# A 128-byte pad ahead of the difference tiles of the four late seven-product stages of a hybrid encoder block

## The chip, the cores and the metric

The kernel runs on one core of a Trainium2 chip. The metric is device time in microseconds (us), the median of several executions. One more execution was recorded by the hardware profiler; every row of a trace below is of that one, and places in it are given in us from its first instruction. The engines are TensorE (PE in the rows; its weight loads are PEld), VectorE (DVE), ScalarE (ACT), GpSimd (POOL) and SyncE (SP, which issues most transfers).

## The reference

One encoder layer over 1024 positions of 1024 channels, with 16 learned meta positions ahead of them, all in float32:

```
u = rms_norm(h, pre_w)
z = u @ w_in                          # 1024 x 7680: q, k, v, gates of both branches
y_r = gated(retention(rq, rk, rv), rg) @ w_ret_branch
y_a = gated(window_attention(aq, ak, av), ag) @ w_attn_branch
out = (sigmoid(gr) * y_r + sigmoid(ga) * y_a) @ w_out
return h + rms_norm(out, post_w)
```

Retention is bidirectional over chunks of 128 with 4 heads; attention sees a window of 128 on both sides, the meta positions and a learned sink.

## The kernel before, in words

**Precision.** Every operand of a large product is held as two tiles, a high part (ScalarE casts it to the fast float32 form) and a low part (VectorE subtracts the high part from the source). The helper `mm3` (lines 93 to 98) makes one product of a 128x128 block out of three matmuls: high weights by high moving data (line 95), low weights by high moving data (line 96), high weights by low moving data (line 97). So a row of line 95, 96 or 97 is one third of a block product, and each of them reads 512 float32 columns, 2048 bytes in each partition, of its moving operand:

```
def mm3(o, ah, al, bh, bl, first, last, free_group=False):
    kw = {"skip_group_check": True} if free_group else {}
    nc.tensor.matmul(o, ah, bh, start=first, stop=False, **kw)
    nc.tensor.matmul(o, al, bh, start=False, stop=False, **kw)
    latest[:] = [nc.tensor.matmul(o, ah, bl, start=False, stop=last, **kw).ins]
```

**Seven products.** The large projections are done in 2x2 blocks with seven products instead of eight. Four of the seven moving operands are plain blocks or a difference kept in the tile `big` (B11, B21, B22 and T1); three are differences of blocks that have tiles of their own, T2, T3 and T4 (`PROD`, line 969). Each of the three has a high and a low tile of 128 partitions by 4 rows (index k) by 512 columns, 8192 bytes in each partition. A product runs four values of k, three matmuls each, so 12 matmuls; units (256 output channels) are taken in pairs, so that the same moving operand serves 24 matmuls in a row, or 12 where pairs are interleaved (`sequence`, line 1166, and `Phase.product`, line 1071).

**Stages.** An early stage `y` (line 1710; the rows have `by`, and its difference tiles are called `T2q`, `T3q` and `T4q`, made by `products`, line 514) runs from about 340 to 500 us. Then comes attention, with single products of the next stage as filler between its steps (rows `pe`). The four late stages follow one another in `steps` (line 1477): `z` (rows `bz`; the remaining gate projections, 12 units), `r` (rows `br`; the retention branch's projection, 4 units), `a` (rows `ba`; the attention branch's, 4 units) and `o` (rows `bo`; the output projection, 4 units). All four use one set of T2, T3 and T4 tiles, which are filled anew for each: by transfers that bring back what stage `y` stored (`get_sum`, line 1178), by ScalarE and VectorE (`split_b`, line 1662, called from `refill`, line 1188), or by transfers of sums that were made earlier (`get_pre`, line 1174).

**What sets the order.** `run` (line 1272) prepares the weights (`lh`, `ll`) up to six products ahead; each engine's instructions are in one fixed order, settled when the program is built. VectorE adds the products up out of PSUM (rows `c1`, `u2`, `u3`, `c5`; line 1111), applies factors (lines 1323, 1362), and makes the low parts (line 111).

**Where the tiles lie.** After attention its pools are closed, and three pools are opened on the space that they leave. `gp` has the buffers of fetched data and of small results (`gtile`, line 981: six buffers of 2048 bytes, and eight small ones for the last norm); `yt`, right behind it, has the six difference tiles:

```
yp, gp, yt = (ctx.enter_context(tc.tile_pool(name=n, bufs=1, reuse_waits="tile")) for n in ("yp", "gp", "yt"))
for n in ("T2", "T3", "T4"):
    B[n] = [yt.tile([P, 4, 512], R, name=f"{n}{s}")[:, :, :] for s in range(2)]
for n in ("T2", "T3", "T4"):
    get_sum(n)
    next(steps)
```

The built program gives each tile a byte address, the same in every partition. The tiles that the argument is about are these (s = 0 is the high tile, s = 1 the low one; the four k rows of a T tile lie 2048 bytes apart, so all four have the same remainder):

| tile | address of s = 0 | address of s = 1 | remainder mod 256 |
|---|---|---|---|
| T2 (stages z, r, a, o) | 122720 | 130912 | 96 |
| T3 | 139104 | 147296 | 96 |
| T4 | 155488 | 163680 | 96 |
| T4q (stage y) | 131040 | 139232 | 224 |
| T3q | 147424 | 155616 | 224 |
| T2q | 163808 | 172000 | 224 |
| big, B11 | 6816 | 40096 | 160, then 224, 32, 96 with k |
| weights, high and low, of stage y and of the late stages | 172000 and up | 184288 and up | 224 |

Of the kernel before, what the change touches and what calls it, by code (L numbers as in the profile page):

```python
# [7 lines left out]
F32 = mybir.dt.float32  # L8
# [8 lines left out]
P = 128  # L17
# [39 lines left out]
def block_kernel(ctx: ExitStack, tc: tile.TileContext, xT, x, meta, w_in, w_rb, w_ab, w_out, vecs, dec, sink,  # L57
# [1743 lines left out]
    rope_stack.close()  # L1801
    free.extend(["p1", "p1", "p3"])
    yp, gp, yt = (ctx.enter_context(tc.tile_pool(name=n, bufs=1, reuse_waits="tile")) for n in ("yp", "gp", "yt"))
    for n in ("T2", "T3", "T4"):
        B[n] = [yt.tile([P, 4, 512], R, name=f"{n}{s}")[:, :, :] for s in range(2)]
    for n in ("T2", "T3", "T4"):
# [86 lines left out]
```

## Time and profile before

| | us |
|---|---|
| median of 3 executions | 1047.75 |
| lowest and highest of them | 1047.32, 1048.1 |
| the profiled execution's own time | 1047.21 |
| its span, first to last instruction | 1045.4 |

The span is what the rows add up to; 1.8 us of the profiled execution lie around it. The granted TensorE clock is 0.996 of full speed on average. In the windows view, a stretch of the span is followed by each engine's busy time in it with the number of instructions, then the granted clock (PEclk), the mean busy share of the DMA engines and GB/s. A row of the timeline has the start and the duration of one instruction. Matmuls are pipelined: each lasts about 0.39 us in the rows, though the next one starts some 0.23 us after it, so what a matmul costs is read from the distance between starts, not from its duration. I call that distance the **step**.

### The profile page before, as it was taken

The page shows a single profiled execution, that of the slowest core. Times are in us where ns is not written, and L with a number is a line of the kernel's source. Part 1 is how long each engine was busy: PE and PEld are TensorE (multiplying, and loading weights), DVE is VectorE, ACT ScalarE, POOL GpSimd, SP SyncE. Part 2 cuts the span into 40 slices and gives each one's busy share as a digit, 9 for nine tenths or more (in the row PEclk, how much of TensorE's full clock was granted, in tenths as well). Part 3 has the DMA queues.
Part 4 walks back from the last instruction along what each step waited for, and adds up shares of the span by engine and source line. Part 5 has one row for each costly group of instructions (what it writes and reads, how often), then busy time and mean ns, then how long its engine had stood idle before and what let it go on. Part 6 is the DMA issues. An engine that isn't in the chain of part 4 may idle for free. (4 is left out here: it accounts for less than half of the span.)

```text
span 1045.4 us, 17242 instructions
## 1 busy us (share of the span) xinstructions
PE 1028.3 (98%) x5797; PEld 892.6 (85%) x5797; DVE 844.4 (81%) x1739; ACT 511.9 (49%) x1118; POOL 210.1 (20%) x274
## 2 busy tenths in 40 slices
PE   9999999999999999999899999999999999999997
PEld 8998999989999888888699898888888888787886
DVE  7887788779889787895877886699899799768766
ACT  5641441423435643433677776476567355333432
POOL 4424235235233002331023331000000000111030
PEclk9999999999999999999899999999999999999999
DMA  9322211215244399997976784999889747789472
GB/s 342 156 81 91 82 42 51 72 36 197 77 142 143 120 409 323 267 290 231 325 215 215 240 248 150 361 382 344 301 291 345 243 137 256 207 227 323 108 139 101
DMA packets 117961, 217.17 MB, mean 208 GB/s; under 512 B 12704, under 2 KB 44352, under 8 KB 115280
## 3 DMA queue, kind: packets, MB, share of 16 engines
q1 hardware_dynamic: 112144, 206.09, 57.3%
q0 software_dynamic: 5440, 9.44, 6.1%
q8 instruction: 46, 0.75, 0.3%
q10 hardware_dynamic: 288, 0.53, 0.2%
q14 instruction: 43, 0.35, 0.1%
HBM read 142.57 MB, written 75.55 MB: 209 GB/s over the span
## 5 line engine op out<-in xcount | busy, mean ns | idle before, releaser
L95 PE MATMUL pv<-wh,big 128*128 128x256 f32 x256 | 73.3, 286 | 0.0
L96 PE MATMUL pv<-wh,big 128*128 128x256 f32 x256 | 72.9, 285 | 0.0
L97 PE MATMUL pv<-wl,big 128*128 128x256 f32 x256 | 72.5, 283 | 0.0
L1548 POOL TENSOR_SCALAR p<-p,den 128x352 f32<-128x352 f32 (+2 forms) x56 | 36.3, 661 | 126.2 <-DVE den L1541 53.0
L1371 POOL DMA_DIRECT2D mx_d<-c1a x4 | 3.5, 872 | 287.3 <-DVE c1a L1362 287.3
L95 PE MATMUL bz<-T,lhz 128*128 128x512 f32 x144 | 56.8, 395 | 0.0
L96 PE MATMUL bz<-T,llz 128*128 128x512 f32 x144 | 56.8, 394 | 0.0
L97 PE MATMUL bz<-T,lhz 128*128 128x512 f32 x144 | 56.8, 394 | 0.0
L1014 ACT CAST why<-wry 128x512 fp32r<-128x512 f32 x56 | 33.0, 620 | 47.3 <-PE by L97 26.2
L96 PE MATMUL by<-big,wly 128*128 128x512 f32 x128 | 50.7, 396 | 0.0
L95 PE MATMUL by<-big,why 128*128 128x512 f32 x128 | 50.4, 394 | 0.0
L97 PE MATMUL by<-big,why 128*128 128x512 f32 x128 | 50.4, 393 | 0.0
L96 PEld LDWEIGHTS pv<-wh,big 128*128 128x128 f32 x256 | 48.2, 188 | 0.3
L95 PEld LDWEIGHTS pv<-wh,big 128*128 128x128 f32 x256 | 48.2, 188 | 0.2
L97 PEld LDWEIGHTS pv<-wl,big 128*128 128x128 f32 x256 | 48.3, 189 | 0.2
L1463 POOL DMA_DIRECT2D aq_d<-m_aq x32 | 27.2, 1278 | 104.0 <-DVE u3y L1458 66.1
L111 DVE TENSOR_TENSOR wly<-wry,why 128x512 fp32r<-128x512 f32 x56 | 38.0, 694 | 11.3 <-ACT why L1014 11.2
L1538 ACT ACTIVATE p<-raw,nm 128x353 f32<-128x353 f32 (+2 forms) x64 | 36.2, 567 | 15.5 <-DVE nm L1535 14.6
L596 ACT ACTIVATE op<-pa,rcol 128x256 f32<-128x256 f32 x32 | 15.3, 477 | 41.9 <-PE pa L97 41.6
L658 ACT ACTIVATE ost<-to,rnw 128x128 f32<-128x128 f32 x64 | 20.1, 366 | 31.4 <-PE to L653 21.8
L1535 DVE CUSTOM_DVE_ANT_0 raw<-ps,mask,nsink 128x352 f32<-128x352 f32 (+2 forms) x64 | 33.2, 548 | 2.7 <-ACT p L1538 1.9
L689 POOL TENSOR_TENSOR rs<-rs,mhalf 128x1 f32<-128x1 f32 x32 | 23.3, 727 | 52.5 <-DVE rs L688 49.2
(715 smaller groups left out, 3768.0 us busy)
## 6 DMA issues: line engine op xcount, KB each, us to landing
e<-e SPq DMA_DIRECT2D x60, 256.0 KB, 5.2
we<-in_w_in_dram SPq DMA_DIRECT2D x20, 512.0 KB, 5.5
wr<-in_w_in_dram SPq DMA_DIRECT2D x19, 512.0 KB, 4.2
wry<-in_w_in_dram SPq DMA_DIRECT2D x16, 512.0 KB, 6.9
tg<-tg_d SPq DMA_DIRECT2D x32, 256.0 KB, 5.0
T<-tT SPq DMA_DIRECT2D x6, 1024.0 KB, 10.3
T<-preT SPq DMA_DIRECT2D x6, 1024.0 KB, 7.1
wrz<-in_w_in_dram SPq DMA_DIRECT2D x20, 256.0 KB, 5.3
```

The lines of the kernel that those rows point to most:

```text
L95: nc.tensor.matmul(o, ah, bh, start=first, stop=False, **kw)
L96: nc.tensor.matmul(o, al, bh, start=False, stop=False, **kw)
L97: latest[:] = [nc.tensor.matmul(o, ah, bl, start=False, stop=last, **kw).ins]
L111: return nc.vector.tensor_tensor(o, i, hi.bitcast(F32), ALU.subtract).ins
L596: nc.scalar.activation(o, pa[:, 0:256], AF.Copy, scale=rcol[:, c:c + 1])
L658: nc.scalar.activation(ost[0][:, e_, w0:w0 + P], to[:, P * e_:P * e_ + P], AF.Copy, scale=rnw[:, 2 * h + e_:2 * h + e_ + 1])
L689: nc.gpsimd.tensor_tensor(rs, rs, mhalf[:, 0:1], ALU.pow)
L1014: nc.scalar.copy(h, src)
L1463: nc.gpsimd.dma_start(d[a], m2[b], accum_op=ALU.add)
L1535: nc.vector.tensor_tensor_reduce(raw[e_][:, 1:1 + wid], s[:, 0:wid], mask[:, mo:mo + wid], -SCALE, nsink[:, hp:hp + 1], ALU.add, ALU.min, ...
L1538: last["exp"] = nc.scalar.activation(p[:, 0:1 + wid], raw[e_][:, 0:1 + wid], AF.Exp, scale=-1.0, bias=nm_[:, e_:e_ + 1], accum_out=den[:, ...
L1548: nc.gpsimd.tensor_scalar(pt[e_][:, 0:wid], pt[e_][:, 0:wid], den[:, e_:e_ + 1], 1.0, op0=ALU.mult, op1=ALU.mult)
```

## The change

One tile of 128 bytes in each partition is taken from the pool `gp` ahead of everything else in it. Nothing reads or writes it.

```
@@ -1801,6 +1801,7 @@
     rope_stack.close()
     free.extend(["p1", "p1", "p3"])
     yp, gp, yt = (ctx.enter_context(tc.tile_pool(name=n, bufs=1, reuse_waits="tile")) for n in ("yp", "gp", "yt"))
+    gp.tile([P, 32], F32, name="pad")
     for n in ("T2", "T3", "T4"):
         B[n] = [yt.tile([P, 4, 512], R, name=f"{n}{s}")[:, :, :] for s in range(2)]
     for n in ("T2", "T3", "T4"):
```

In the built program the change moves no instruction: all five engines have the same instructions in the same order, with the same waits for the same counts. What differs is the address of 20 buffers, each 128 bytes higher: the six buffers of `gtile` (110176 to 120416 before, 110304 to 120544 now), the eight small ones behind them, and the six difference tiles. Those start now at 122848, 131040 (T2), 139232, 147424 (T3), 155616 and 163808 (T4), all at 224 mod 256. Five of these six are, to the byte, the starts of tiles of T2q, T3q and T4q in the table above. The weights, `big`, the tiles of the other pools and everything in PSUM stay where they were.

More of the change, by code (lines that the diff above doesn't have):

```diff
@@ L1803, in block_kernel @@
     yp, gp, yt = (ctx.enter_context(tc.tile_pool(name=n, bufs=1, reuse_waits="tile")) for n in ("yp", "gp", "yt"))
+    gp.tile([P, 32], F32, name="pad")
     for n in ("T2", "T3", "T4"):
```

## Prediction

> **What bounds the kernel now.** I read the page first, then the waits of PE from 660 us to the end, where the four late stages lie, then the windows.
>
> ```profile
> span 1045.4 us, 17242 instructions
> PE 1028.3 (98%) x5797; PEld 892.6 (85%) x5797; DVE 844.4 (81%) x1739; ACT 511.9 (49%) x1118; POOL 210.1 (20%) x274
> ```
> ```profile
> PE bo L95 <- ACT lho L1014: 0.8, 1, 0.8
> ```
> ```profile
> 700.00:740.00 40.00, 40.00 (x174) 32.41 (x173) 36.89 (x61) 22.96 (x43) 0.00 (x0) 1.00 0.96 330
> 780.00:820.00 40.00, 40.00 (x174) 32.40 (x173) 36.18 (x60) 27.51 (x51) 0.00 (x0) 1.00 0.96 338
> 846.00:892.00 46.00, 46.00 (x199) 37.09 (x199) 45.98 (x77) 26.36 (x48) 0.00 (x0) 1.00 0.55 180
> ```
>
> From 660 us on PE has a single listed wait, 0.8 us. In the windows (PE, PEld, DVE, ACT, POOL, then the clock) PE is busy throughout at clock 1.00. So matmuls set the end there, and only what changes the step between matmuls can change the time. The third window is special: DVE is busy for 45.98 of 46.00 us, so there DVE sets the pace too.
>
> **How many matmuls read the moved tiles.** The groups with `T` as moving operand, line 95 (lines 96 and 97 have the same counts):
>
> ```profile
> L95 PE MATMUL bz<-T,lhz 128*128 128x512 f32 x144 | 56.8, 395 | 0.0
> L95 PE MATMUL br<-T,lhr 128*128 128x512 f32 x48 | 18.9, 394 | 0.0
> L95 PE MATMUL ba<-T,lha 128*128 128x512 f32 x48 | 18.9, 394 | 0.0
> L95 PE MATMUL bo<-T,lho 128*128 128x512 f32 x44 | 17.2, 394 | 0.0
> ```
>
> That is 3 x (144 + 48 + 48 + 44) = 852. The durations say nothing of the step, so I take starts from the timeline. First the tiles as they lie now (96 mod 256): the first, eleventh and last row of a run of T matmuls in stage z, and the `big` row behind a run.
>
> ```profile
> 719.21 0.39 PE L95 MATMUL bz<-T,lhz 128*128 128x512 f32 x1
> 721.53 0.40 PE L96 MATMUL bz<-T,llz 128*128 128x512 f32 x1
> 727.58 0.39 PE L95 MATMUL bz<-big,lhz 128*128 128x512 f32 x1
> ...
> 763.81 0.39 PE L95 MATMUL bz<-T,lhz 128*128 128x512 f32 x1
> 772.21 0.39 PE L95 MATMUL bz<-big,lhz 128*128 128x512 f32 x1
> ```
>
> The first run has 36 matmuls. Its first ten take 2.32 us, a step of 232 ns; the other 26 take 6.05 us, a step of 232.7 ns. Another run of 36 takes 8.40 us, 233.3 ns each. Now stage y, whose tiles lie at 224 mod 256, where the change puts the late ones:
>
> ```profile
> 403.45 0.39 PE L95 MATMUL by<-T3q,why 128*128 128x512 f32 x1
> 405.76 0.39 PE L96 MATMUL by<-T3q,wly 128*128 128x512 f32 x1
> 408.94 0.39 PE L95 MATMUL by<-big,why 128*128 128x512 f32 x1
> ...
> 491.78 0.39 PE L95 MATMUL by<-T4q,why 128*128 128x512 f32 x1
> 494.50 0.40 PE L97 MATMUL by<-big,why 128*128 128x512 f32 x1
> ```
>
> Here the first ten of the T3q run of 24 take 2.31 us, 231 ns each, and the other 14 take 3.18 us, 227 ns each. The T4q run of 12, which follows a single `big` matmul, takes 2.72 us, 226.7 ns each from its first on. So these tiles have a shorter step, after some ten matmuls in which it settles. Over all rows of T2q to T4q from 350 us to 494 us, counted by their place in the run, the first ten average 230.1 ns and the later ones 226.7. The late T rows, from 674.59 to 1035.32 us, average 232.0 and 232.6.
>
> The clock and the transfers do not separate the two (windows of PE alone: busy time, clock, DMA share, GB/s):
>
> ```profile
> 403.45:408.94 5.49, 5.49 (x26) 1.00 1.01 328
> 719.21:727.58 8.37, 8.37 (x38) 1.00 1.02 369
> ```
>
> The clock is 1.00 and the DMA share 1.01 and 1.02. The matmuls' shape and the remainder of the weights' addresses are alike too. What differs is the start of the moving operand, and the change makes that equal: five of the six tiles come to lie on the very bytes of T?q tiles. The peculiar pace of each address I can't explain, only read.
>
> **The sum.** A T matmul at its eleventh place or later should save 232.6 - 226.7 = 5.9 ns. One of the first ten should save 232.0 - 230.1 = 1.9 ns; the two runs shown bound that by 1.0 (231 against 232) and 5.3 (226.7 against 232). Counted so, 423 of the 852 are late in their run and 429 early: 423 x 5.9 + 429 x 1.9 = 3.3 us if nothing takes it back. Two stretches do.
>
> The first is 846 to 893 us:
>
> ```profile
> DVE llr L111 <- PE br L96: 1.3, 1, 1.3
> ```
> ```profile
> PEld ba L96 <- DVE lla L111: 0.7, 2, 0.4
> ```
>
> DVE last waits for PE at 846.02 (first row), and is then busy without a gap until PE waits for it near 889 and 892 (second row). What PE gains before 846 it carries in, since DVE's start there hangs on a PE matmul; what it gains inside becomes a longer wait at 892. The second is the start of stage o:
>
> ```profile
> DVE sto0S L1042 <- DMA wro<-mx_d: 1.5, 1, 1.5
> ```
> ```profile
> 943.65 0.68 DVE L1111 TENSOR_TENSOR c1a<-c1a,ba 128x512 f32<-128x512 f32 x1
> 949.62 1.94 SPq L1385 DMA_DIRECT2D wro<-mx_d  x2
> ```
>
> PE's 0.8 us wait near 960 is for weights that come through DRAM. The chain to them begins with the sum at 943.65, made from a PE product, goes through an accumulating transfer, and ends in the load issued at 949.62. So what PE gains between 943.6 and 960 is waited away there. In these two stretches lie 51 + 67 of the T matmuls' early and late places. There remain 356 x 5.9 + 378 x 1.9 = 2.1 + 0.7 = **2.8 us**. The early places' bounds make it 2.5 to 4.1. `big` runs that follow T runs settle afresh too, and I take nothing for that; runs behind T?q and behind T average within 0.6 ns of one another over twelve matmuls, which is at most 0.3 us over some 40 such runs, so I round up to 2.9. The 24 half-width matmuls of the last product are left at nothing: if they too went down by 5.9 in 232.6 they would give 0.07 us. The tail behind them is DVE, POOL and transfers, and stays.
>
> **The other moved buffers.** DVE and ACT read and write the six buffers of `gtile` and the difference tiles. DVE's low parts written at 96 mod 256 and at 224:
>
> ```profile
> L111 DVE TENSOR_TENSOR T<-z,T x12: 692/696/702, 792.9 to 809.1; 128x512 fp32r<-128x512 f32 x12
> L111 DVE TENSOR_TENSOR T4q<-x,T4q x4: 684/685/687, 356.4 to 358.8; 128x512 fp32r<-128x512 f32 x4
> ```
>
> 696 ns against 685 is, if anything, in favour of the new place; it would count only in the DVE-bound stretch, where 12 such rows give 0.13 us. I take nothing; with the sign reversed it is 0.13 us against, both inside the range. No DMA is added, moved or resized, no wait is added.
>
> TensorE: Matmul & The Clock Gate, in the Trainium skill, section "Back-to-back issue gap", gives the warm gap as N / 2.4 + 2.5 ns, 216 ns at N = 512 by its formula, with no term for where the operand lies. By that page this change would do nothing. The steps of 232.7 and 226.7 ns above differ at one shape and one clock, which the rule does not allow for, so I give its result the small chance of rival 1.
>
> **Rivals.**
>
> 1. *The address is not the cause.* Stage y differs from the late stages in more than the T tiles: other weight pools, other neighbours in time. Then the step stays near 232.6 and the time 1047.75. Against it: the `big` runs keep one rhythm in both parts, and the difference begins and ends with the T?q tiles.
> 2. *DVE or DMA takes most of it.* If DVE paced the stages before 846 as well, only what is gained after 893 and outside the second stretch would stay: 104 late and 126 early places, 0.85 us, which gives 1046.9. For it: 36.89 and 36.18 of 40 us in the windows above, and a DMA share of 0.96. Against it: DVE idles 3 to 4 us in each of these, and PE never waits.
> 3. *Slower: the new place locks into a long rhythm.* The step is a rhythm, and one tile can have two: the T runs above went at 232.5 and at 233.3. The longest that I find over twelve matmuls is this:
>
> ```profile
> 339.47 0.40 PE L97 MATMUL by<-big,why 128*128 128x512 f32 x1
> 342.29 0.39 PE L97 MATMUL by<-big,why 128*128 128x512 f32 x1
> ```
>
> Twelve matmuls in 2.82 us, 235.0 ns. If runs in the late stages, cut by `big` matmuls, stayed in such a rhythm, 852 x 2.5 = 2.1 us would be added: 1049.9. It turns slower once the mean step over the T rows is above 232.5. Against it: every T?q run of 24 settles below 228.
>
> **How the numbers follow.** The profiled execution took 1047.21, 0.54 below the median of the runs, 1047.75. The saving of 2.9 makes 1044.3 of it, and 1044.85 of the median: I say 1044.8. The forecast has a chance of 0.76, rival 1 of 0.10, rival 2 of 0.10, rival 3 of 0.04. The forecast's own range is 1043.6 (the upper bound 4.1) to 1045.3 (2.5); up to 1046.9 it reaches rival 2, and leaves out rivals 1 and 3 and the forecast's fringe. About 0.2%, 2.1 us, is what a measurement of this kernel can tell from no change, so faster means below 1045.65: 0.75, nearly all of the forecast. Within 0.2% are rivals 1 and 2 and a remainder of the forecast, 0.21; slower is rival 3, 0.04.
>
> **What would show it.** Right: the T runs of 24 and 36 in the late stages settle at about 227 ns after some ten matmuls, with `big` runs as before; the waits near 892 and 960 grow by a few tenths; the last matmul ends some 2.9 us earlier. The reason is wrong if T steps stay at 232 to 233 (rival 1), or if they fall and new PE waits before 846 take it (rival 2). The sum is wrong if the early places save much more or less than 1.9 ns, because that depends on what ran before.

## The result and the profile after

| | before | after |
|---|---|---|
| median of 13 executions, us | 1047.75 | 1045.01 |
| the profiled execution's own time, us | 1047.21 | 1045.42 |
| its span, us | 1045.4 | 1043.6 |

The ratio of after to before is 0.9974, with a 95% interval of 0.9964 to 0.9985: 2.7 us less, between 1.6 and 3.8.

The head of the page of after and the waits of PE from 660 us on (engine and line, what it waited for, us in total, times, longest):

```profile
span 1043.6 us, 17242 instructions
PE 1025.3 (98%) x5797; PEld 891.9 (85%) x5797; DVE 844.3 (81%) x1739; ACT 511.7 (49%) x1118; POOL 209.0 (20%) x274
```
```profile
PE bo L95 <- ACT lho L1014: 1.2, 2, 1.1
```

The counts are the same, PE's busy time is 3.0 us less, and the listed wait, 0.8 us in one place before, is 1.2 us in two. The windows of after (us of PE, PEld, DVE, ACT, POOL, then the clock, DMA share, GB/s):

```profile
700.00:740.00 40.00, 40.00 (x176) 32.82 (x175) 37.25 (x61) 23.60 (x45) 0.00 (x0) 1.00 0.96 337
846.00:892.00 46.00, 45.86 (x199) 36.78 (x198) 45.97 (x77) 26.29 (x49) 0.00 (x0) 1.00 0.57 184
```

In the first, 176 matmuls fit where 174 did, at the same clock and DMA share. In the second, DVE is busy throughout as before, the count is still 199, and PE, which had no gap, now has 0.14 us of one. The timeline of after, the run of 36 T matmuls that begins at 719.21 us (first, eleventh, and the `big` row behind it):

```profile
719.21 0.39 PE L95 MATMUL bz<-T,lhz 128*128 128x512 f32 x1
721.50 0.39 PE L96 MATMUL bz<-T,llz 128*128 128x512 f32 x1
727.39 0.39 PE L95 MATMUL bz<-big,lhz 128*128 128x512 f32 x1
```

The first ten take 2.29 us (229 ns each; 232 before) and the other 26 take 5.89 us (226.5 ns each; 232.7 before).

For the whole, I add up the distances between starts from the first late T row to the last matmul, below called the stretch. These are the two rows in before and in after:

```profile
674.59 0.39 PE L95 MATMUL bz<-T,lhz 128*128 128x512 f32 x1
1038.32 0.29 PE L97 MATMUL bo<-T,lho 128*128 128x256 f32 x1
```
```profile
675.19 0.39 PE L95 MATMUL bz<-T,lhz 128*128 128x512 f32 x1
1036.46 0.28 PE L97 MATMUL bo<-T,lho 128*128 128x256 f32 x1
```

| part of this stretch | before | after | saved, us |
|---|---|---|---|
| 429 T matmuls at places 1 to 10 of their run, mean step | 232.03 ns | 230.28 ns | 0.75 |
| 423 at later places | 232.57 ns | 226.68 ns | 2.49 |
| 696 512-wide `big` matmuls | 232.25 ns | 231.97 ns | 0.20 |
| half-width matmuls, total | 2.76 us | 2.75 us | 0.01 |
| long steps (over 262 ns): what they have above 232 ns | 1.39 us | 2.39 us | -1.00 |
| the stretch | 363.72 us | 361.27 us | 2.45 |

So 3.45 us is won on steps and 1.00 given back in waits. The spans differ by only 1.8 us because the first T row came 0.60 us later in this execution of after. Nothing ahead of it was changed. Over the kernels of this study that row lies anywhere from 672.9 to 677.4 us, so below I compare this stretch rather than spans.

### The profile page after: what moved, and what is told of

The parts are those of the page before. It is cut to its first block, busy times and chain, and to the rows that moved or that the text cites. A ratio compares the mean times of both kernels' runs of the same rounds, so it can differ in the third digit from the quotient of the medians.

```text
span 1043.6 us, 17242 instructions
## 1 busy us (share of the span) xinstructions
PE 1025.3 (98%) x5797; PEld 891.9 (85%) x5797; DVE 844.3 (81%) x1739; ACT 511.7 (49%) x1118; POOL 209.0 (20%) x274
```

## The experiments

The theory of the prediction was that the start of the moving operand sets the step. Its rivals were that stage `y` is quick for another reason, and that the buffers of `gp`, which move with T, have a part in it.

### Each half of the change alone

T alone, and the buffers of `gtile` alone:

```
     for n in ("T2", "T3", "T4"):
+        if {'T2': 128, 'T3': 0, 'T4': 0}[n]:
+            yt.tile([P, {'T2': 128, 'T3': 0, 'T4': 0}[n] // 4], F32, name=f"pad{n}")
         B[n] = [yt.tile([P, 4, 512], R, name=f"{n}{s}")[:, :, :] for s in range(2)]
```
```
     yp, gp, yt = (ctx.enter_context(tc.tile_pool(name=n, bufs=1, reuse_waits="tile")) for n in ("yp", "gp", "yt"))
+    gp.tile([P, 1], F32, tag="ms1", bufs=4, name="first")
```

> The pad of 128 bytes lies ahead of T2 in yt: only the six difference tiles move, to 224 mod 256; the buffers of gp stay. Theory (the start address of the moving operand sets PE's step): T matmuls settle at 226.7 ns as in the changed kernel, and the time is 2.7 us (0.26%) under before, ratio 0.997 to 0.998. Rival (the moved gp buffers, which VectorE, ScalarE and the transfers use, bring the gain): T steps stay at 232.6 and the ratio is 1.000.

> One of the small buffers of the last norm is taken first from gp, so the six buffers of gtile move up by 128 bytes and the difference tiles stay at 96 mod 256. Theory (moving operand's start): T steps stay at 232 to 233 ns, ratio 1.000 within 0.1%. Rival (gp buffers): the gain of 0.26% appears here, ratio 0.997.

T alone took 1043.53 us against 1047.13, ratio 0.9965 (0.9952 to 0.9978). The buffers alone took 1047.43, ratio 0.9999 (0.9989 to 1.0008). With T alone the stretch is 361.27 us, that of after to the hundredth. With the buffers alone it is 364.29, 1.94 of it in long steps, and the T steps are those of before (232.07 ns at places 1 to 10, 232.55 at later ones). A run of 24 with T alone (first, eleventh, and the one behind the last):

```profile
721.45 0.39 PE L95 MATMUL bz<-T,lhz 128*128 128x512 f32 x1
723.74 0.39 PE L96 MATMUL bz<-T,llz 128*128 128x512 f32 x1
726.91 0.39 PE L95 MATMUL bz<-T,lhz 128*128 128x512 f32 x1
```

Fourteen matmuls in 3.17 us are 226.4 ns each. The whole gain is the move of T.

### Other starts of T, in the kernel

```
+        if {'T2': 32, 'T3': 32, 'T4': 32}[n]:
+            yt.tile([P, {'T2': 32, 'T3': 32, 'T4': 32}[n] // 4], F32, name=f"pad{n}")
```

> Three pads of 32 bytes put T2 at 128, T3 at 160 and T4 at 192 mod 256; gp and everything else stay. Theory: the settled step of the T matmuls differs by tile, one value for each remainder, and is the same in all four stages; T3 at 160 near the 231 to 233 ns that big rows have there. Whether 128 and 192 are short like 224 or long like 96 isn't fixed by the theory. Rival (something other than the remainder, e.g. the very bytes): all three tiles have one step, 232.6 or 226.7.

One execution, 1048.25 us, with a stretch of 363.89. Its runs of 24 settle on average at 234.3 ns (T2, at 128 mod 256), 233.3 (T3, at 160) and 233.3 (T4, at 192). None of the three starts is quick, and 128 is the slowest. Two of them in rows (eleventh, and behind the last), T2 and T3:

```profile
722.41 0.40 PE L96 MATMUL bz<-T,llz 128*128 128x512 f32 x1
725.69 0.39 PE L95 MATMUL bz<-T,lhz 128*128 128x512 f32 x1
...
828.65 0.39 PE L96 MATMUL br<-T,llr 128*128 128x512 f32 x1
831.91 0.40 PE L95 MATMUL br<-T,lhr 128*128 128x512 f32 x1
```

3.28 us over 14 are 234.3 ns; 3.26 us are 232.9, a little under the average of the T3 runs.

### TensorE alone, and the weights moved too

The layer is replaced by groups of 36 matmuls of the kernel's kind (12 triples, two weights tiles, two moving tiles, all in fp32r, the fast float32 form); 40 groups with the weights at 224 mod 256 and other moving starts, then 16 in which the weights' start varies:

```
    for off in range(0, 64, 2):
        group(off, 24)
    for off in range(1, 64, 8):
        group(off, 24)
    for w in range(0, 64, 8):
        group(0, w)
    for w in range(0, 64, 8):
        group(32, w)
```

> Leaves out the layer: 56 groups of 36 matmuls alone on PE, 512 columns, in the order high, high, low of the kernel, with no other engine at work. The first 40 groups differ in the start of the moving operand (8-byte steps through 256 bytes, then odd words), the last 16 in the start of the weights with the moving operand at 128 and at 0 mod 256. Theory: the settled step is a function of the moving start mod 256 alone, 226.7 ns at 224 and 232.3 at 96, and doesn't change with the weights' start. Rival 1 (traffic of other engines makes the difference): one step for all groups. Rival 2 (weights and moving operand meet at some address relation): the step changes in the last 16 groups too.

The mean step of the second half of a group (18 matmuls), in ns, by the moving start less the weights' start, mod 256:

| difference, bytes | 0 | 32 | 64 | 96 | 120 | 128 | 160 | 192 | 224 |
|---|---|---|---|---|---|---|---|---|---|
| weights at 224, moving start varied | 226.7 | 233.3 | 228.9 | 233.3 | 240.0 | 232.5 | 234.1 | 233.3 | 233.3 |
| moving at 128, weights varied | 227.1 | 232.8 | 228.8 | 233.1 | | 232.9 | 234.2 | 233.4 | 233.2 |
| moving at 0, weights varied | 227.1 | 232.8 | 228.8 | 233.5 | | 233.4 | 234.4 | 233.4 | 233.2 |

The table has the multiples of 32, and 120. The first 40 groups go in steps of 8 bytes, with eight more starts between: of those not in the table none is under 230.0 ns (at differences of 56, 104 and 248), and there is 240.0 again at 100 and 240.1 at 132. A difference of 4 has 236.7. So only zero gives 226.7.

The rows of three groups, each at its 19th matmul and at the first of the next group: moving 224 and weights 224; moving 128 and weights 128; moving 88 and weights 224.

```profile
113.57 0.62 PE L36 MATMUL acc<-hi,wt 128*128 128x512 f32 x2
117.65 0.64 PE L36 MATMUL acc<-hi,wt 128*128 128x512 f32 x2
...
349.23 0.62 PE L36 MATMUL acc<-hi,wt 128*128 128x512 f32 x2
353.32 0.62 PE L36 MATMUL acc<-hi,wt 128*128 128x512 f32 x2
...
239.03 0.40 PE L36 MATMUL acc<-hi,wt 128*128 128x512 f32 x1
243.35 0.40 PE L36 MATMUL acc<-hi,wt 128*128 128x512 f32 x1
```

4.08 us, 4.09 us and 4.32 us over 18 matmuls: 226.7, 227.2 and 240.0 ns. A moving start of 128, slow in the kernel at 234.3, is as quick as 224, within 0.5 ns, once the weights lie at 128 too. So it is not the moving start that counts but its **difference** to the weights' start (rival 2 of the expectation); the prediction saw only one of the two because all weights of the stages that it compared lie at 224. And it is TensorE's own doing, since nothing else runs here: the steps of the kernel at 96 (232.6), 128 (234.3), 160 (233.3), 192 (233.3) and 224 (226.7) are found again within 0.3 ns.

### The weights moved to T, in the kernel

This is the direct test: T stays where it was before, and the late weights come down to it by 128 bytes.

```
     with tc.issue_after(softmax[-3]), tc.issue_after(softmax[-1]):
         next(steps)
+    lp.tile([P, 32], F32, name="padw")
     next(i)
```

> The kernel before, with a pad of 128 bytes ahead of the late stages' weights and none ahead of T: T stays at 96 mod 256, and the late weights go from 224 to 96. The 512-wide big matmuls change places among themselves only: each group still has one quarter of its matmuls at each of the differences 0, 64, 128 and 192. Theory of the difference (moving start less weights' start, from the run with TensorE alone): T comes to difference 0, its late steps are 226.7 ns as in the run with the pad ahead of T alone, and the time is 1043.5 to 1045.0. Rival, the moving start alone, as the prediction had it: T has not moved, its steps stay at 232 to 233 and the time at 1047.1 to 1047.8.

It took 1044.45 us against 1047.48, ratio 0.9972 (0.9957 to 0.9987). A run of 24 (first, eleventh, behind the last), and the ends of the stretch:

```profile
672.86 0.40 PE L95 MATMUL bz<-T,lhz 128*128 128x512 f32 x1
...
716.83 0.39 PE L95 MATMUL bz<-T,lhz 128*128 128x512 f32 x1
719.10 0.39 PE L96 MATMUL bz<-T,llz 128*128 128x512 f32 x1
722.27 0.39 PE L95 MATMUL bz<-T,lhz 128*128 128x512 f32 x1
...
1034.10 0.28 PE L97 MATMUL bo<-T,lho 128*128 128x256 f32 x1
```

3.17 us over 14 are 226.4 ns, with T at 96. The stretch is 361.24 us. The theory of the difference holds, and the moving start alone is refuted. The inside of the sum differs: T averages 227.4 ns (228.5 after the change), since its runs settle sooner here, `big` averages 232.85 (231.97), and the long steps hold 2.68 us (2.39). These cancel. Why `big` is slower here, with the same four differences in the same numbers, stays open.

### All differences at zero

If the difference were all, one could do the same for `big`, whose rows start 64 bytes further with each k. Rows of T and of the late weights get that pitch too, which needs the room of the sixth weights buffer. A control gives up that buffer alone, on the changed kernel; its products then follow one another in a somewhat different order (368 T matmuls at places 1 to 10, 484 later):

```
-    LEAD = 6
+    LEAD = 5
```

and the other kernel has this besides, on the kernel before:

```
-                h, l = (lp.tile([P, 4, P], R, tag=t, bufs=LEAD, name=f"{t}{self.nm}{u}_{p}") for t in ("lh", "ll"))
+                h, l = (lp.tile([P, 4, P + 16], R, tag=t, bufs=LEAD, name=f"{t}{self.nm}{u}_{p}")[:, :, 0:P] for t in ("lh", "ll"))
...
+    lp.tile([P, 16], F32, name="padw")
...
+        yt.tile([P, 16], F32, name="pad")
...
-        B[n] = [yt.tile([P, 4, 512], R, name=f"{n}{s}")[:, :, :] for s in range(2)]
+        B[n] = [yt.tile([P, 4, 528], R, name=f"{n}{s}")[:, :, 0:512] for s in range(2)]
```

> The changed kernel with five weights buffers of each kind in place of six; no start of T, weights or big changes its remainder. It is the control for the next kernel, which needs the room of the sixth buffer. Both theories expect the steps of the changed kernel (T 226.7 late, big 232.0), and 1045.0 if the sixth buffer is spare; if the preparation of the weights runs closer to its use, some waits of TensorE for weights and up to 1047.

> Rows of the late weights and of T get a pitch that is 64 mod 256 (16 unused elements behind each of the four parts), as the rows of big have it already, with five weights buffers. Part k of the weights, of T and of big then start at the same remainder, so that every 512-wide matmul of the four late stages has difference 0. Theory of the difference: T and big both step at 226.7 ns, without a settling of ten matmuls at the change from one to the other. Against the kernel with five buffers that is 792 x (232.0 - 226.7) = 4.2 us for big and some 430 x (230 - 226.7) = 1.4 us for the early places of T, less some tenths in each DVE-bound stretch: 1039.5 to 1041.5 if that kernel takes 1045. Rival, the moving start alone: only moving starts at 224 are quick; three quarters of the T and big rows now lie elsewhere, T loses what it won and big stays: 1047 to 1048.

Both missed. The control took 1051.58 us (ratio 1.0035, 1.0018 to 1.0053): its steps are those of after (T 228.5, `big` 231.9), but its long steps hold 8.56 us in 18 places, where after has 2.39 in 7. The largest of PE's waits in it, 1.2 us in after:

```profile
PE bo L95 <- ACT lho L1014: 3.4, 2, 2.7
```

So the sixth buffer is not spare: it saves some 6 us. The kernel with all differences at zero took 1051.05 us (1.0024, 1.0008 to 1.0040), no better than its control by what these can tell. T and `big` both have the same middling step, 231.5 and 231.4 ns: T loses 2.6 us on it against the control, which 1.9 us less in long steps (6.68) and 0.4 on `big` nearly make up for. A T run of 24:

```profile
719.89 0.40 PE L95 MATMUL bz<-T,lhz 128*128 128x512 f32 x1
722.20 0.39 PE L96 MATMUL bz<-T,llz 128*128 128x512 f32 x1
725.45 0.40 PE L95 MATMUL bz<-T,lhz 128*128 128x512 f32 x1
```

231 ns in the first ten, 232 in the rest: it never settles. Its single steps repeat 237, 232, 230, 224, 231, 236 through the run. A difference of zero is then not enough. What this kernel has and the quick ones lack is that both starts change every third matmul.

### Three more differences, in the kernel

```
-            rows[r] = (gp.tile([P, 3], F32, tag="ms2", bufs=4, name=f"ms2_{r}"), [], [])
+            rows[r] = (gp.tile([P, 4], F32, tag="ms2", bufs=4, name=f"ms2_{r}"), [], [])
...
-            m1.append(gp.tile([P, 1], F32, tag="ms1", bufs=4, name=f"ms1_{r}"))
+            m1.append(m2[:, 3:4])
...
+        if {'T2': 32, 'T3': 32, 'T4': 32}[n]:
+            yt.tile([P, {'T2': 32, 'T3': 32, 'T4': 32}[n] // 4], F32, name=f"pad{n}")
```

> T2 at 0, T3 at 32 and T4 at 64 mod 256 in the late stages, weights at 224 (a column of another small tile is used in place of a tile, so that T can move down; nothing is left out). That is differences of 32, 64 and 96. If the run with TensorE alone holds for the kernel, runs of T2 settle at 233.3 ns, T3 at 228.9 and T4 at 233.3; the time lies near 1047. If DVE, ACT and DMA traffic shape the step, the three differ from that.

One execution, 1049.29 us, above the expected 1047; but its stretch, 363.74, is that of before (363.72), and what lies outside it made the rest. The eleventh row of a run of 24 and the one behind its last, for T2 (difference 32) and T3 (64):

```profile
723.45 0.40 PE L96 MATMUL bz<-T,llz 128*128 128x512 f32 x1
726.72 0.39 PE L95 MATMUL bz<-T,lhz 128*128 128x512 f32 x1
...
829.29 0.39 PE L96 MATMUL br<-T,llr 128*128 128x512 f32 x1
832.49 0.39 PE L95 MATMUL br<-T,lhr 128*128 128x512 f32 x1
```

3.27 and 3.20 us over 14: 233.6 and 228.6 ns; T4 (96) has 233.0. With TensorE alone they were 233.3, 228.9 and 233.3. Again the other engines and the transfers have no visible part in the settled step of T.

### Starts that turn, other widths, another type

The layer is left out again. `m` and `w` give the moving and the weights' offset of the i-th matmul of a group of 48; `turn(o)` goes round four starts o elements apart, one per triple:

```
    for o in (16, 32, 8):
        group(turn(o), turn(o))
    group(turn(16, 1), turn(16, 1))
    group(turn(16), at(0))
    group(at(0), turn(16))
    group(turn(16), turn(16, 3, 1))
    group(lambda i: 48 if i % 13 == 12 else 0, at(0))
```

> Leaves the layer out: 42 groups of 48 matmuls alone on TensorE, 27 of them and the last in fp32r as in the kernel (groups of three with the same k; width 512, then 256 and 384), 14 in bf16. The theory that only the difference of the two starts counts needs 226.7 ns wherever it is 0, also where weights and moving operand turn together by 64, 128 or 32 bytes every three matmuls. The kernel with a pitch of 64 for T and weights speaks against that (231.5 at difference 0 throughout), unless traffic of other engines did it. The rival is that the quick rhythm has to settle: it needs starts that stay, and each change of start throws it back. Then turning groups stay at 230 to 233 with TensorE alone too; a group whose every 13th matmul has another moving start is thrown back each time (about 229); and groups with starts that stay at 160, 192, or moving starts 256 and 512 bytes further on, settle at 226.7. For width 256 and for bf16 nothing is measured yet: if the address acts as it does here, their steps differ by start by some ns too; if not, by less than 0.5.

| fp32r, 512 wide | step, ns |
|---|---|
| both starts stay, difference 0 (at 128, 160 or 192; moving start 256 or 512 bytes further) | 226.7 |
| both turn by 64, 128, 32 bytes per triple, difference 0 | 231.7, 234.4, 231.7 |
| both turn by 64 bytes with every matmul, difference 0 | 228.3 |
| the moving start alone turns by 64 (as `big` in the kernel) | 231.7 |
| the weights' start alone turns by 64 | 231.7 |
| both turn by 64, the weights one matmul behind (differences 0 and 64) | 231.7 |
| every 13th matmul at another moving start | 228.9 |

Two rows of the group in which both turn by 64, 24 matmuls apart, and two of one in which both stay:

```profile
28.89 0.62 PE L40 MATMUL acc<-mv,wt 128*128 128x512 f32 x2
34.45 0.62 PE L40 MATMUL acc<-mv,wt 128*128 128x512 f32 x2
...
117.57 0.61 PE L40 MATMUL acc<-mv,wt 128*128 128x512 f32 x2
123.01 0.61 PE L40 MATMUL acc<-mv,wt 128*128 128x512 f32 x2
```

5.56 us is 231.7 ns a matmul, 5.44 us is 226.7. The rival of this expectation holds in the main: 226.7 ns was seen only with a difference of zero and starts that stay (in their remainder mod 256). This fits the settling of T after `big`, and `big` at about 232 in the kernels, since its start changes every third matmul. It is not the whole account. If each change threw the rhythm back by ten matmuls, starts that turn with every matmul could not be quicker (228.3) than those that turn with every third (231.7). And how long a run takes to settle depends on what ran before it: in after, the first ten of a T run average from 226.6 to 231.5 ns where no wait falls among them. What sets the rhythm in turning groups stays open.

Other shapes, by difference. Here the weights keep one start and the moving start takes seven, so these rows don't tell whether the difference or the moving start alone counts:

| shape | lowest | highest |
|---|---|---|
| fp32r, 256 wide | 113.3 ns (192) | 120.0 ns (0 and 96) |
| fp32r, 384 wide | 173.3 ns (0, 32, 64, 224) | 176.7 ns (96) |
| bf16, 512 wide | 215.8 ns (all seven) | 215.8 ns |
| bf16, 256 wide | 109.2 ns (all seven) | 109.2 ns |

Two rows each, 24 matmuls apart, of fp32r 256 wide at differences 0 and 192, and of bf16 512 wide at 128:

```profile
158.59 0.52 PE L40 MATMUL acc<-mv,wt 128*128 128x256 f32 x3
161.47 0.52 PE L40 MATMUL acc<-mv,wt 128*128 128x256 f32 x3
186.98 0.50 PE L40 MATMUL acc<-mv,wt 128*128 128x256 f32 x3
189.70 0.51 PE L40 MATMUL acc<-mv,wt 128*128 128x256 f32 x3
...
337.32 0.59 PE L40 MATMUL acc<-mb,wb 128*128 128x512 bf16 x2
342.50 0.59 PE L40 MATMUL acc<-mb,wb 128*128 128x512 bf16 x2
```

2.88 and 2.72 us: 120.0 and 113.3 ns. At 256 wide, zero is among the worst differences. The bf16 group takes 5.18 us, 215.8 ns a matmul, and so do the other six. That is the value which the Trainium skill, TensorE: Matmul & The Clock Gate, section "Back-to-back issue gap", gives for this width by its formula for an isolated matmul; the formula holds here for streams of bf16 at every start tried, and for fp32r at none. The 131 ns that the same section gives for a sustained stream at this width is met by no step here. The weight loads (group rows of the same run, mean ns of one) differ between the types:

```profile
L40 PEld LDWEIGHTS acc<-mv,wt 128*128 128x128 f32 x1344 | 226.4, 190 | 38.6 <-ACT mv L28 9.8
L40 PEld LDWEIGHTS <-wb 128*128 128x128 bf16 x672 | 65.7, 98 | 43.4 <-issue 0.2
```

A load of fp32r weights lasts 190 ns, and of bf16 weights 98. The mean of the first mixes the three widths. That a long weight load gets in the way of the moving operand's reads, depending on where both start, would fit the bf16 rows and the part that the weights' start plays; the runs do not show it, and it stays open.

## Why the prediction was right, and what was incomplete in it

**What bounds the kernel** (matmuls, through their step): right. A change of nothing but starts moved the end, and the steps, less what the waits took back, explain it.

**The late places, 5.9 ns each**: 5.89 measured. **The early places, 1.9 ns**: 1.75. **The `big` runs behind T**: taken at 0.1 us by rounding, 0.20 measured. **The half-width matmuls**, left at nothing: 0.01. In the kernel they take 120.17 ns before and 119.65 after, so next to no gain was to be had there. (TensorE alone has 120.0 at a difference of 0, as after, but 118.5 at 128, where T lay before; why the kernel is 1.6 ns slower there stays open.)

**The two stretches that take it back**: named rightly, and in this execution priced too low. The places left out for them were worth 0.5 us by the prediction's own prices (51 x 1.9 + 67 x 5.9 ns); the long steps grew by 1.00. Around 887 to 893 us they grew from 0.32 to 0.61 us, as expected by some tenths. At the start of stage o they grew from 1.07 to 1.78. The rows there, before and then after:

```profile
960.44 0.50 PE L95 MATMUL bo<-big,lho 128*128 128x512 f32 x1 [0.80 <-ACT lho L1014]
```
```profile
957.50 0.49 PE L95 MATMUL bo<-big,lho 128*128 128x512 f32 x1 [0.18 <-ACT lho L1014]
959.06 0.50 PE L95 MATMUL bo<-big,lho 128*128 128x512 f32 x1 [1.06 <-ACT lho L1014]
```

The first wait is new, the second longer. The chain ahead of them in after, the sum, the load and the load's landing (transfers view: KB each, median us from issue to landing; before's row first):

```profile
941.75 0.68 DVE L1111 TENSOR_TENSOR c1a<-c1a,ba 128x512 f32<-128x512 f32 x1
947.71 2.43 SPq L1385 DMA_DIRECT2D wro<-mx_d  x2
```
```profile
wro<-mx_d SPq DMA_DIRECT2D x2, 512.0 KB, 9.0
```
```profile
wro<-mx_d SPq DMA_DIRECT2D x2, 512.0 KB, 9.5
```

Sum and load both came 1.9 us earlier (943.65 and 949.62 before), so up to here the chain followed PE in full, as the prediction had it. Then the load took 0.5 us longer to land, and that is about half of the 1.00 us given back. Whether the quicker steps cause it is not shown. The same load landed after 9.6 us in the kernel that moves only the buffers, whose long steps hold 1.94 us, and after 8.5 us with T at 128, 160 and 192, where they hold 0.79; so it varies by as much without any gain in the steps. In the two other kernels with T at difference zero and nothing else changed it took 9.5 us (T alone moved) and 9.8 (the weights alone), and one execution of each can't weigh that.

**The sum**: 2.9 us foreseen, 2.45 in the rows of the stretch, 2.7 between the medians. The 0.5 us at the start of stage o is what separates the first two.

**The other moved buffers**, taken at nothing: ratio 0.9999.

**The rivals**: rival 1 (the address is not the cause) falls with the kernels that move T alone and the weights alone. Rival 2 (DVE takes it before 846) falls with the 176 matmuls against 174 in the window 700 to 740, and with the waits: none is listed for PE from 660 us on but those of stage o. Rival 3 (a slower rhythm at the new place) falls with the runs at 226.5; that there are slower places, up to 240.1, is shown by TensorE alone.

**The reason** was the incomplete step of the prediction. It said that what differs is the start of the moving operand. The weights at 96 make T at 96 quick, and T at 128 is quick or slow with the weights at 128 or 224. The forecast held because the weights' remainder was alike, which the prediction had noted without seeing that it counts. Had the change moved the weights by the same 128 bytes, the reason as put would have foreseen this gain all the same, and by the difference there would be none; that was not run. "The peculiar pace of each address" is this difference; that of `big` goes with starts that do not stay.

No version was found that beats the change: T alone (361.27 us of stretch) and the weights moved to T (361.24) do the same by another pad. A pitch of 4352 bytes for `big`, which would let its start stay, was not tried: the tiles of the early stages then need more memory than there is.

## What to carry to other kernels

Where a kernel is bound by a long stream of fp32r matmuls, read the step from the starts of rows, run by run, and compare it with the byte starts of both operands: at 512 columns, equal remainders mod 256 that stay over a run gave 226.7 ns, others 228.9 to 240.1, and a pad sets them. The best start changes with the width (at 256 columns the moving start 192 bytes beyond that of the weights), and bf16 had no such dependence on the moving start. When steps shrink, look next at weights that come through DRAM or from a busy DVE: in the profiled execution 1.00 of the 3.45 us won went into such waits.

## What the runs showed of the hardware

- The step of fp32r matmuls depends on (moving start less weights' start) mod 256 with nothing else running: 226.7 ns at 0, 228.9 at 64, 232.5 to 234.4 at the other multiples of 32, 230.0 to 240.1 between them. Moving starts 256 and 512 bytes further on changed nothing. In the kernel the settled steps of T agree within 0.4 ns.
- The quick rhythm takes up to some ten matmuls to settle, by what ran before, and is not held where starts turn, those of either operand: both turning by 64 bytes per triple gives 231.7 ns at a difference of zero, with every matmul 228.3.
- At 256 columns, with the weights at one start, the order is another: 113.3 ns at 192 and 120.0 at 0 and 96.
- The Trainium skill, SBUF — State Buffer, section "Who interferes with whom", gives PE one read port for the moving operand and one for weights, independent, and says that PE never waits on anyone. Of other engines the trace agrees: the settled steps of T in the kernel and alone differ by at most 0.4 ns. If independent means that the two reads are without influence on one another, fp32r does not bear it out (226.7 to 240.1 ns by the difference of their starts); by bf16 alone, 215.8 ns throughout, one would not see it.
